# A two-layer transformer kernel: free distances between the stages of a written-out order, and stacking transfers issued by GpSimd

## The chip, the core and the metric

The kernel runs on one core of a Trainium2 chip. The metric is the device time of one execution in microseconds (us). TensorE multiplies matrices, VectorE and ScalarE do elementwise work, SyncE issues nearly all the transfers, and GpSimd does very little in the kernel before. In the profile these are PE (with PEld for its weight loads), DVE, ACT, SP and POOL.

## What is computed

The reference is a transformer of two layers on a sequence of 256 tokens with 1024 features, all in float32. Per layer:

```python
h = _rmsnorm(x, norm_attn[layer]); proj = h @ w_in[layer]      # 1024 x 2956
o_sb = stick_breaking_attention(...)     # 4 heads
o_mb = moba_attention(...)               # 4 heads
o_ns = nsa_attention(...)                # 4 heads: compressed, selected and window branch
o_df = diff_attention(...)               # 4 heads, difference of two softmaxes
x = x + concatenate([o_sb, o_mb, o_ns, o_df]) @ w_out[layer]
h2 = _rmsnorm(x, norm_mlp[layer])
x = x + square(relu(h2 @ w_up[layer])) @ w_down[layer]         # 1024 x 4096 x 1024
```

and a last norm after both layers.

## The kernel before, in words

**Precision.** A float32 number is split into a high part, rounded to the fast matmul type, and the low part that is left. A product takes three matmuls: high by high, high by low, low by high. Each weight piece of 1 MB is loaded into a buffer (`wraw`, three of them), split by ScalarE (`whi`) and VectorE (`wlo`), in halves, and multiplied.

**Stages of a layer** (`attention`, lines 1137 to 1193; `out_proj` 1225; `mlp` 1251). Six projections (`proj`: vg, sqk, nqk, dqk, v2, mqk) come one after another, and the four kinds of attention (`stick`, `nsa`, `diff`, `moba`) are woven between them, one unit of work per head. Each unit is cut into stages by `yield`: scores, softmax, transposes, product with V, split for the output product. Then come `out_proj` (four pieces of `w_out`) and the MLP, 16 rounds of up and down.

**Stacking.** Scores need a high and a low part of 64 rows stacked on the 128 partitions, or other arrangements of them. `stack2` (lines 896 to 902) makes one by four transfers from SBUF to SBUF, 64 partitions by 2 KB each, issued by SyncE: three stacks after sqk (12 transfers), one after nqk (4), three after mqk (12), so 28 a layer and 56 in all. `stack3` (line 883), for `diff`, goes through HBM and stays on SyncE.

**The order is written out beforehand.** No call goes to the machine directly. `Order.note` records each with a clock (`at` sets it), `link` finds what depends on what, and `schedule` (lines 348 to 459) plays the program through a small model of the engines (a cost for each operation from `estimate`, line 212) in which every engine takes, of the calls that are ready, the one with the lowest clock. The order that comes out is what each engine's queue gets, and each queue runs in that order. So the clocks are priorities: `START` (line 27) for the units of each head, `LOADS` and `LEADS` for loading and splitting each weight piece, `FIRST` for the first norm, and `STAGE = 1.2`, by which `run` (line 848) raises the clock from one stage of any unit to the next. `choose` (line 360) lets SyncE's next call block its queue when its buffer isn't free.

**Start.** SyncE loads x, the identity and the gains, and then the first weights. GpSimd sets a few constants. `setup_consts`, `setup_bias` and `setup_small` (lines 562 to 626) load small tables at the clock of the projection that they stand beside.

**The compressed branch.** `compress` (line 1004) leaves one tile `VC` of 128 x 64 whose four groups of 32 partitions hold the same values; in `nsa` (line 1099) head h multiplies 32 partitions of it with 32 partitions of `PcT`, a product that uses 32 rows of the array.

Of the kernel before, what the change touches and what calls it, by code (L numbers as in the profile page):

```python
# [26 lines left out]
START = {  # L27
    "sb": ((-2128.1, -135.2, -1435.8, 37.9), (-286.7, -731.7, -641.4, 39.7)),
    "ns": ((27.1, -1051.7, 53.8, 45.5), (48.2, -2101.2, 32.8, -175.5)),
    "cw": ((-1062.2,), (-2120.7,)),  # L30
    "cmp": ((-1801.8,), (-695.1,)),
    "df": ((-1887.0, -3174.2, -1854.8, -2205.7), (24.0, -2246.5, 53.7, 52.7)),
    "mb": ((-87.3, -1433.6, -45.1, -356.5), (-276.0, -1568.2, -350.0, -7140.8)),
}

LOADS = (
# [6 lines left out]
)  # L43
LEADS = (
# [17 lines left out]
)  # L62
CW_LOAD = 41.5
STAGE = 1.2

FIRST = (-100.5, -617.1)
# [63 lines left out]
GAP, DRAIN = 13.0, 94.0  # L130

SLOW_RATE = 200.0

WINDOW, BUSY_COLUMNS = 10240 / 3, 3060
LOOK_AHEAD, MARGIN = 0.75, 1.0
SPARE = {"ps": 2}

# [40 lines left out]
class Order:  # L178
# [33 lines left out]
    def estimate(op, eng, method, writes, reads):  # L212
        o, n = writes[0], _columns_of(writes[0])
        if method == "dma_start":
            op.bytes = 4 * n * o.ap[0][1]
            if _space(o) == SBUF and (_space(reads[0]) == SBUF or "scratch" in reads[0].tensor.name) and o.ap[0][1] <= 64:
                op.bytes *= DMA_RATE / SLOW_RATE
            return 650.0 if _space(o) == _space(reads[0]) == SBUF else 475.0
# [129 lines left out]
    def schedule(self):  # L348
# [9 lines left out]
        dma, now = 0.0, 0.0  # L358

        def choose(e):  # L360
            skipped, pick = [], None
            while ready[e] and pick is None:
# [7 lines left out]
                if ok and not self.buffers(op, held):  # L370
                    ok = False
                    if e == "SP":
                        skipped.append(x)
                        break
# [36 lines left out]
        while len(done) < len(ops):  # L411
# [9 lines left out]
            for e in ENGINES:  # L421
# [8 lines left out]
                if op.bytes:  # L430
                    dma = max(dma, op.end + DMA_START) + op.bytes / DMA_RATE
                    op.end = dma + DMA_SEEN
# [51 lines left out]
def trunk(ctx: ExitStack, tc: tile.TileContext, x, w_in, w_out, w_up, w_down, gattn, gains, pos, cw1, cw2,  # L484
# [50 lines left out]
    nc.sync.dma_start(gn, gains)  # L535
    for f in range(2):
        nc.sync.dma_start(xs[:, 1, f * 512:(f + 1) * 512], xv[:, 1, f * 512:(f + 1) * 512])
    at(-100.0)

    half = cp.tile([128, 1], F32, name="half")  # L540
# [5 lines left out]
    negone = cp.tile([128, 128], F32R, name="negone")  # L546
    nc.gpsimd.memset(F(negone), -1.0)
# [5 lines left out]
    KC = [cp.tile([128, 2, 16], F32R, name=f"KC{i}") for i in range(2)]  # L553
    w2 = cp.tile([128, DEPTH, 2, 2, 64], F32, name="w2")
# [832 lines left out]
```

## Time and profile before

| | |
|---|---|
| median of 3 runs | 649.02 us (647.96 to 649.22) |
| the profiled execution | 648.43 us, of which the span from first to last instruction is 646.7 us |
| PE busy | 622.2 us, 96% of the span |
| DVE, ACT, POOL busy | 441.7, 358.9 and 8.3 us |
| DMA | 126.94 MB, 196 GB/s on average |

The span is that of the profiled execution, and the 1.73 us around it are taken as fixed. A matmul's end is modelled, so that short pauses between matmuls do not show as idle time: busy time is an upper bound of the work. A busy array isn't an array at its peak either.

### The profile page before, as it was taken

What the parts mean: (1) busy time and instruction counts of PE and PEld (TensorE: products, weight loads), DVE (VectorE), ACT (ScalarE), POOL (GpSimd) and SP (SyncE); (2) the same over time, 40 slices, a digit from 0 to 9 for tenths busy, and PEclk for the clock granted to TensorE, in tenths of its full rate; (3) what the DMA queues carried; (4) which work ended last, traced back from release to release, by engine and by line L of the source; (5) the groups of instructions that cost most, each with busy time, mean ns of one, the idle gap of its engine ahead of it and who ended that gap; (6) DMA issues with size and microseconds to landing.
All of it is one profiled execution on the core that took longest, in us unless ns stands there. A gap on an engine that the chain in (4) does not pass through costs nothing.

```text
span 646.7 us, 9744 instructions
## 1 busy us (share of the span) xinstructions
PE 622.2 (96%) x3674; PEld 529.0 (82%) x3674; DVE 441.7 (68%) x900; ACT 358.9 (56%) x693; POOL 8.3 (1%) x25
## 2 busy tenths in 40 slices
PE   5989999999999999999999999999999999999995
PEld 4978768788888888888889977887788888888885
DVE  5749579779576566556686674998866666576466
ACT  5547587566455454445364774776744454454453
POOL 2010000000000000000000000000000000000000
PEclk9999999999999999999999999999999999999999
DMA  7787955844354465555636958446355555545531
GB/s 275 254 246 227 273 196 222 255 148 176 122 215 155 176 256 186 199 192 196 212 112 222 276 222 235 190 126 236 127 196 195 196 199 191 197 162 196 196 130 66
DMA packets 26895, 126.94 MB, mean 196 GB/s; under 512 B 3880, under 2 KB 5928, under 8 KB 14048
## 3 DMA queue, kind: packets, MB, share of 16 engines
q1 hardware_dynamic: 26848, 126.32, 57.0%
q8 instruction: 29, 0.48, 0.3%
q14 instruction: 18, 0.15, 0.1%
HBM read 115.79 MB, written 3.17 MB: 184 GB/s over the span
## 4 chain that ended last, share of the span: by engine, by line
PE 75%; DMA 9%; DVE 8%; ACT 5%; issue 1%; SPq 1%; POOLq 0%; POOL 0%; ACTq 0%; DVEq 0%
PE ps L480 75%; DMA wraw<-in_w_in_dram 3%; DVE wlo L480 3%; DVE t L480 2%; ACT t L480 2%; ACT whi L480 2%; DMA wraw<-in_cw_dram 2%; DVE xs L480 1%; DMA cst<-in_cst_dram 1%; DMA s<-qtl 1%; DMA wraw<-in_w_down_dram 1%; DVE x L480 1%; SPq L480 1%; DMA t<-bias_scratch 1%; ACT x L480 1%
## 5 line engine op out<-in xcount | busy, mean ns | idle before, releaser
L480 DVE TENSOR_TENSOR wlo<-wraw,whi 128x1024 fp32r<-128x1024 f32 (+1 forms) x192 | 231.2, 1212 | 109.6 <-ACT whi L480 93.7
L480 ACT ACTIVATE whi<-wraw 128x1024 fp32r<-128x1024 f32 (+1 forms) x192 | 199.8, 1049 | 147.0 <-PE ps L480 111.3
L480 PE MATMUL ps<-x,whi 128*128 128x256 f32 (+1 forms) x1024 | 212.7, 341 | 0.7 <-DVE x L480 0.7
L480 PEld LDWEIGHTS ps<-x,whi 128*128 128x128 f32 x1024 | 153.8, 190 | 15.9 <-issue 1.2
L480 PE MATMUL ps<-whi,t 128*128 128x512 f32 (+1 forms) x528 | 162.6, 385 | 0.3 <-ACT whi L480 0.3
L480 PEld LDWEIGHTS ps<-x,wlo 128*128 128x128 f32 x768 | 112.9, 190 | 12.0 <-issue 0.6
L480 PE MATMUL ps<-x,wlo 128*128 128x256 f32 x768 | 122.0, 283 | 0.1
L480 PEld LDWEIGHTS ps<-whi,t 128*128 128x128 f32 x528 | 97.8, 188 | 20.1 <-ACT whi L480 1.0
L480 PE MATMUL ps<-wlo,t 128*128 128x512 f32 (+1 forms) x264 | 101.0, 385 | 0.0
L480 ACT ACTIVATE t<-ps 128x256 f32<-128x256 f32 (+1 forms) x109 | 44.1, 413 | 45.9 <-PE ps L480 45.1
L480 PEld LDWEIGHTS ps<-wlo,t 128*128 128x128 f32 x264 | 49.7, 188 | 9.5 <-DVE wlo L480 0.2
L480 ACT ACTIVATE t<-t 128x512 fp32r<-128x512 f32 (+5 forms) x53 | 29.3, 552 | 35.4 <-DVE t L480 33.6
L480 ACT ACTIVATE t<-t,sm 128x128 f32<-128x128 f32 (+1 forms) x98 | 42.2, 443 | 10.7 <-DVE sm L480 10.4
L480 DVE TENSOR_TENSOR t<-ps,t 128x256 f32<-128x256 f32 x64 | 26.7, 421 | 28.0 <-ACT t L480 27.3
L480 PE MATMUL ps<-whi,x 128*128 128x512 f32 (+1 forms) x128 | 36.0, 384 | 1.0 <-ACT x L480 1.0
L480 DVE TENSOR_TENSOR t<-t,t 128x512 fp32r<-128x512 f32 (+2 forms) x44 | 27.4, 622 | 8.0 <-ACT t L480 6.9
L480 DVE CUSTOM_DVE_ANT_0 t<-ps,Bt 128x256 f32<-128x256 f32 (+1 forms) x80 | 24.4, 352 | 9.0 <-PE ps L480 9.0
L480 PEld LDWEIGHTS ps<-whi,x 128*128 128x128 f32 x128 | 23.1, 193 | 4.7 <-ACT x L480 1.5
L480 PE MATMUL ps<-whi,mixh 128*128 128x512 f32 (+1 forms) x68 | 26.7, 397 | 0.0
L480 PE MATMUL ps<-whi,mixl 128*128 128x512 f32 (+1 forms) x68 | 26.5, 389 | 0.0
L480 PE MATMUL ps<-wlo,mixh 128*128 128x512 f32 (+1 forms) x68 | 26.3, 386 | 0.0
L480 DVE SCALAR_TENSOR_TENSOR t<-t 128x512 f32<-128x512 f32 (+1 forms) x36 | 22.9, 635 | 1.0
(139 smaller groups left out, 475.1 us busy)
## 6 DMA issues: line engine op xcount, KB each, us to landing
wraw<-in_w_up_dram SPq DMA_DIRECT2D x32, 1024.0 KB, 4.8
wraw<-in_w_down_dram SPq DMA_DIRECT2D x32, 1024.0 KB, 4.8
wraw<-in_w_in_dram SPq DMA_DIRECT2D x20, 1024.0 KB, 4.9
wraw<-in_cw_dram SPq DMA_DIRECT2D x8, 1024.0 KB, 9.4
wraw<-in_w_out_dram SPq DMA_DIRECT2D x8, 1024.0 KB, 6.6
s<-qth SPq DMA_DIRECT2D x28, 128.0 KB, 4.3
s<-qtl SPq DMA_DIRECT2D x28, 128.0 KB, 3.2
wraw<-in_w_in_dram SPq DMA_DIRECT2D x4, 792.0 KB, 6.7
```

Source lines behind the costliest of these rows:

```text
L480: fn(*a, **k)
```

## The change

1. All the clocks are replaced by new ones. Instead of one `STAGE` for all, `STAGES` gives a distance, of either sign, for each stage of each head of each kind and layer. `CW_LOAD` has one value a layer, and `SETUP` gives the small loads distances of their own.
2. `stack2` issues its transfers on GpSimd's queue.
3. The model: a DMA issue on GpSimd costs 1000 ns (on SyncE 650 ns for one inside SBUF), each issuing engine has a DMA queue of its own, the least gap between matmuls is 14 ns, and SyncE may look past four calls whose buffers aren't free.
4. Eleven matmuls of `negone` with zeros stand at the head of PE's queue; `negone` and the zeros are set by VectorE.
5. `VC` becomes a tile of four blocks, block h zero outside of partitions 32h to 32h+31, so that the product takes all 128 rows; four copies make it instead of one.

```diff
-CW_LOAD = 41.5
-STAGE = 1.2
+CW_LOAD = (41.5, 48.9)
+
+STAGES = {
+    "sb": (((108.7, -127.7, 154.5, 212.1, 2.6), (56.3, -117.1, -134.2, 119.8, 55.1), (-73.1, 224.1, -250.0,
...
+}
+
+SETUP = (
+    -43.2, -25.2, -92.3, -41.0, -227.3, 245.8, 3.6, 22.9, -207.8,
+)
...
-GAP, DRAIN = 13.0, 94.0
+GAP, DRAIN = 14.0, 94.0
...
+POOL_DMA = 1000.0
...
+WARM = 11
...
+        if method == "dma_start" and eng == "POOL":
+            op.bytes = 4 * n * o.ap[0][1] * DMA_RATE / SLOW_RATE
+            return POOL_DMA
...
-        dma, now = 0.0, 0.0
+        dma, now = dict.fromkeys(ENGINES, 0.0), 0.0
...
-                    if e == "SP":
+                    if e == "SP" and len(skipped) == 4:
                         skipped.append(x)
                         break
...
-                    dma = max(dma, op.end + DMA_START) + op.bytes / DMA_RATE
-                    op.end = dma + DMA_SEEN
+                    dma[e] = max(dma[e], op.end + DMA_START) + op.bytes / DMA_RATE
+                    op.end = dma[e] + DMA_SEEN
...
+    at(-1000.0)
+    negone = cp.tile([128, 128], F32R, name="negone")
+    nc.vector.memset(F(negone), -1.0)
+    at(-100.0)
...
+    at(-1000.0)
+    p, w = ps_att(), t2(F32R)
+    nc.vector.memset(F(w), 0.0)
+    for i in range(WARM):
+        mm(p, negone, w, i == 0, i == WARM - 1)
+    at(-100.0)
...
+    VC = cp.tile([128, 4, 64], F32, name="VC")
+    nc.gpsimd.memset(VC, 0.0)
...
-    def setup_consts():
+    def setup_consts(clock):
+        at(clock, SETUP[0])
         nc.sync.dma_start(c, cst)
...
-    def setup_bias():
+    def setup_bias(clock):
+        at(clock, SETUP[2])
         tb = ap.tile([32, 12], F32, name="tb")
...
-        for _ in unit(h):
-            clock += STAGE
+        for s, _ in enumerate(unit(h)):
+            clock += STAGES[name][l][h][s]
             at(clock)
...
-                nc.sync.dma_start(F(s[64 * m:64 * m + 64, i]), F(x[order[m]][64 * i:64 * i + 64]))
+                nc.gpsimd.dma_start(F(s[64 * m:64 * m + 64, i]), F(x[order[m]][64 * i:64 * i + 64]))
...
-        VC = ap.tile([128, 64], F32, name="VC", tag="VC", bufs=2)
-        evac(VC, p[:, 0:64])
-        return VC, clock
+        for h in range(4):
+            r = slice(32 * h, 32 * h + 32)
+            evac(VC[r, h], p[r, 0:64])
+        return clock
...
-            av.append((VCs[0][32 * h:32 * h + 32], PcT[32 * h:32 * h + 32], 0))
+            av.append((VC[:, h], PcT, 0))
...
```

## Rows read from the trace of the kernel before

**Rows 1.** The page: busy time by engine, and the chain by engine.
```profile
PE 622.2 (96%) x3674; PEld 529.0 (82%) x3674; DVE 441.7 (68%) x900; ACT 358.9 (56%) x693; POOL 8.3 (1%) x25
...
PE 75%; DMA 9%; DVE 8%; ACT 5%; issue 1%; SPq 1%; POOLq 0%; POOL 0%; ACTq 0%; DVEq 0%
```
**Rows 2.** Busy time of the engines in stretches: attention, MLP, attention, MLP.
```profile
7.40:148.30 140.90, 135.76 (x931) 114.54 (x931) 105.14 (x311) 92.70 (x233) 3.30 (x7) 1.00 0.72 234
148.30:326.40 178.10, 178.10 (x908) 151.09 (x909) 115.06 (x148) 86.13 (x119) 0.55 (x1) 1.00 0.51 185
326.40:461.80 135.40, 130.28 (x930) 112.11 (x928) 101.74 (x284) 89.10 (x215) 0.55 (x1) 1.00 0.65 209
461.80:638.70 176.90, 176.60 (x898) 150.00 (x899) 113.43 (x143) 86.81 (x121) 0.55 (x1) 1.00 0.47 170
```
**Rows 3.** Waits of PE over the span: us in total, times, longest.
```profile
PE ps L480 <- DVE xn L480: 7.4, 1, 7.4
PE ps L480 <- DMA s<-qtl: 2.6, 3, 1.3
PE ps L480 <- DMA wraw<-in_cw_dram: 1.3, 2, 0.7
PE ps L480 <- DVE xs L480: 1.2, 2, 0.6
PE ps L480 <- ACT t L480: 1.0, 1, 1.0
PE ps L480 <- DMA t<-in_hot_dram: 1.0, 1, 1.0
PE ps L480 <- ACT x L480: 1.0, 1, 1.0
```
**Rows 4.** PE's timeline at the first weights: start, us in all, count.
```profile
11.23 1.01 PE L480 MATMUL ps<-whi,x 128*128 128x396 f32 x2
...
14.13 0.88 PE L480 MATMUL ps<-whi,x 128*128 128x396 f32 x4
14.85 0.52 PE L480 MATMUL ps<-wlo,x 128*128 128x396 f32 x2
```
**Rows 5.** Stacking transfers over the span: ns of an issue (least, median, most), and landing.
```profile
L480 SPq DMA_DIRECT2D s<-qth x28: 461/588/607, 33.6 to 434.5; - x28
L480 SPq DMA_DIRECT2D s<-qtl x28: 462/596/1412, 36.2 to 437.6; - x28
...
DMA to landing us min/median/max: 2.2/3.9/7.8
```
**Rows 6.** SyncE's queue at the last group of twelve stacking transfers.
```profile
430.07 1.11 SPq L480 DMA_DIRECT2D s<-qth  x2
...
435.15 3.00 SPq L480 DMA_DIRECT2D s<-qtl  x4
438.25 0.53 SPq L480 DMA_DIRECT2D wraw<-in_w_out_dram  x1
```
**Rows 7.** PE's timeline around there, a product of `VC` (32*64) among it.
```profile
427.15 0.65 PE L480 MATMUL ps<-PcT,VC 32*64 32x256 f32 x4
427.73 0.55 PE L480 MATMUL ps<-ident,t 128*128 128x128 f32 x3
...
438.86 0.47 PE L480 MATMUL ps<-s,s 128*128 128x256 f32 x2 [1.27 <-DMA s<-qtl]
```
**Rows 8.** Groups of POOL: its longest instruction, and a short one.
```profile
L480 POOL CAST msb<-cst 128x256 fp32r<-128x256 f32 x1 | 1.4, 1395 | 0.0
...
L480 POOL MEMSET Bc<- 128x128 f32 x1 | 0.2, 204 | 0.0
```
**Rows 9.** Groups of DVE by shape: splitting weights, and scaling by a column.
```profile
L480 DVE TENSOR_TENSOR wlo<-wraw,whi 128x1024 fp32r<-128x1024 f32 x184 | 223.6, 1222 | 107.9 <-ACT whi L480 92.3 <-PE ps L480 15.2
...
L480 DVE TENSOR_SCALAR t<-t,sm 128x256 f32<-128x256 f32 x25 | 8.5, 349 | 0.1
```
**Rows 10.** The copy that makes `VC`: ns, and its start.
```profile
L480 DVE COPY VC<-ps x1: 219/219/219, 408.1 to 408.1; 128x64 f32<-128x64 f32 x1
```

More of the change, by code (lines that the diff above doesn't have):

```diff
@@ L27 @@
 START = {
[L28 to L33, printed above, removed]
+    "sb": ((-248.9, -199.3, -114.1, -39.1), (-78.6, -144.2, -73.5, -49.7)),
+    "ns": ((-244.9, -201.1, 58.0, 43.6), (34.4, -250.0, -4.8, -16.4)),
+    "cw": ((-111.2,), (-138.7,)),
+    "cmp": ((-199.7,), (-197.7,)),
+    "df": ((-250.0, -232.6, -136.2, -184.4), (16.1, -237.3, 58.0, -100.2)),
+    "mb": ((-250.0, -63.5, -250.0, -176.1), (-36.2, -249.7, -131.0, -248.6)),
 }
 LOADS = (
[6 rows of a table removed]
[6 rows of a table added]
 )
 LEADS = (
[17 rows of a table removed]
-)
-CW_LOAD = 41.5
-STAGE = 1.2
-FIRST = (-100.5, -617.1)
[17 rows of a table added]
+)
+CW_LOAD = (41.5, 48.9)
+STAGES = {
[7 rows of a table added]
+    "cmp": (((111.1, 39.1, 250.0, -250.0, 250.0),), ((-136.0, -178.1, -245.4, 226.4, 250.0),)),
[7 rows of a table added]
+}
+SETUP = (
+    -43.2, -25.2, -92.3, -41.0, -227.3, 245.8, 3.6, 22.9, -207.8,
+)
+FIRST = (-7.7, -250.0)
 LAYER = 300.0
@@ L535, in trunk @@
     nc.sync.dma_start(gn, gains)
+    at(-100.0, SETUP[8])
     for f in range(2):
         nc.sync.dma_start(xs[:, 1, f * 512:(f + 1) * 512], xv[:, 1, f * 512:(f + 1) * 512])
+    at(-100.0)
+    at(-1000.0)
+    negone = cp.tile([128, 128], F32R, name="negone")
+    nc.vector.memset(F(negone), -1.0)
     at(-100.0)
@@ L545, in trunk @@
     nc.gpsimd.memset(G, 0.0)
-    negone = cp.tile([128, 128], F32R, name="negone")
-    nc.gpsimd.memset(F(negone), -1.0)
+    at(-1000.0)
[4 more added lines that the diff above has]
+    at(-100.0)
     tri = cp.tile([128, 128], F32R, name="tri")
@@ L568, in setup_consts @@
             nc.gpsimd.tensor_copy(KC[i], Pc[:, 0, 0, :].rearrange("p (a b) -> p a b", a=2))
+        at(clock, SETUP[1])
         for l in range(DEPTH):
@@ L587, in setup_bias @@
         nc.sync.dma_start(rt, rows)
+        at(clock, SETUP[3])
         p = ps_att()
@@ L593, in setup_bias @@
         nc.sync.dma_start(scr, vb[:12])
+        at(clock, SETUP[4])
         for g in range(6):
@@ L601, in setup_bias @@
             nc.vector.tensor_copy(Bt[:, 2 * g:2 * g + 2, :], rev)
+        at(clock, SETUP[5])
         nc.gpsimd.memset(Bc, 8.0 * NEG)
@@ L604, in setup_bias, with setup_small @@
         nc.vector.tensor_copy(Bc[:, 0, :, 0:7], Bt[:, 4:8, 159:256:16])
-    def setup_small():
+    def setup_small(clock):
+        at(clock, SETUP[6])
         lv = t2()
         nc.sync.dma_start(lv[:, :DEPTH * 128], lamv.to_broadcast([128, DEPTH * 128]))
+        sl = small(2)
+        nc.sync.dma_start(sl, subln)
+        at(clock, SETUP[7])
         d = small(4)
@@ L621, in setup_small @@
                                            e[:, 2 * l + 1:2 * l + 2], op0=ALU.add, op1=ALU.subtract)
-        sl = small(2)
-        nc.sync.dma_start(sl, subln)
         for l in range(DEPTH):
@@ L1151, in attention @@
         if l == 0:
-            setup_consts()
+            setup_consts(clock)
+            at(clock)
         acc, clock = proj(l, "sqk", xT, False, clock)
@@ L1160, in attention @@
         if l == 0:
-            setup_bias()
+            setup_bias(clock)
+            at(clock)
         acc, clock = proj(l, "nqk", xT, False, clock)
@@ L1168, in attention @@
         if l == 0:
-            setup_small()
+            setup_small(clock)
+            at(clock)
         acc, clock = proj(l, "dqk", xT, False, clock)
@@ L1175, in attention @@
         at(clock)
-        VC, _ = compress(l, base + START["cw"][l][0], base + CW_LOAD)
+        compress(l, base + START["cw"][l][0], base + CW_LOAD[l])
         at(clock)
-        VCs[:] = [VC]
         run(cmp, l, "cmp", 0)
@@ L1193, in attention @@
         return mix, clock
-    VCs = []
     def ps_out():
```

59 rows, old and new, of tables (LEADS, LOADS, STAGES) are left out of this document.

## The prediction

> **What bounds the kernel now.** I read the page first. PE is busy for 622.2 of 646.7 us and three quarters of the chain are PE's [rows 1], so only what PE loses can be won, and the 24.5 us in which it shows idle are the first measure of that. POOL, with 8.3 us of work [rows 1], is nearly free to issue transfers.
>
> Next the stretches [rows 2]. The two MLPs run for 178.1 and 176.9 us with 0.0 and 0.3 us of PE idle: the change alters no instruction there, and I give it nothing. The two attention stretches, each with its output product, run 931 and 930 matmuls in 140.9 and 135.4 us, with PE idle for 5.1 us in each. So the same work takes 5.5 us longer in the first layer. Before the first stretch lie 7.4 us in which PE waits for the norm of x, after the last MLP about 8 us of last norm and store; the change touches neither wait.
>
> The waits of PE [rows 3] tell what the idle time is. Waits for `xs` and for the norm's `x` (1.2 and 1.0 us) belong to the boundaries between stages, where nothing else is ready, and stay. What an order or a queue can move is the wait for stacked parts (2.6), for the compression's weights (1.3), for a score's evacuation (1.0) and for the table of buckets (1.0): 5.9 us, and some 0.7 us of smaller ones, so 6.6 us. To this come pauses inside "busy" time, since a matmul's modelled end hides short ones.
>
> The starts of the first matmuls show the clock [rows 4]. From 11.23 to 14.13 eight matmuls of 396 columns start in 2.90 us, 0.36 each; the next four take 0.72 us, 0.18 each. That is 1.2 GHz against 2.4 GHz: PE, idle until 7.41, ran the first 6.7 us of its work at half speed.
>
> **The change part by part.** The sum is made against the profiled execution, 648.43 us; the median of the runs is 0.6 us above it, which I add at the end.
>
> *Eleven matmuls at the start.* 512 columns at half speed are 0.36 x 512/396 = 0.47 us, so 5.1 us in all, beginning once VectorE has written two constants (about 1.3 us after the start, since nothing else waits on VectorE before x lands). They end at about 6.4, before PE is wanted at 7.41, and cost nothing; if they began 1 us later they would begin to. [...] The eight matmuls then need 1.44 instead of 2.90 us, a gain of 1.5 at most there, but ScalarE and VectorE are still splitting x in this stretch. Bounds 0 and 2.9 (the eight, and as much again for transposes before them); I take 0.7, half of the first 1.5.
>
> *Transfers on GpSimd's queue.* Removed from SyncE are 56 issues of 0.59 us [rows 5], 33 us of its time. SyncE isn't short of time, but its queue runs in order: the last group of twelve takes from 430.07 to 438.25, and the load of `w_out` goes out only behind it [rows 6]. Twelve issues also make a chain of 8.2 us, at whose end PE stands still for 1.27 us [rows 7]. On GpSimd the trace before shows no issue. Its instructions take from 0.20 to 1.40 us [rows 8], and the longest stacking issue on SyncE took 1.41 [rows 5], so I bound an issue by 0.2 and 1.4 us. The change's own model puts it at 1000 ns against 650 on SyncE; the ratio times the measured 0.59 gives 0.91, an assumption and no measurement, and it lies inside. I take 0.9. A group of twelve then takes 10.8 us and its last part lands 3.7 us later, counted from the split. Three of the four groups have other matmuls to cover this; the last has none (the wait of 1.27 us is there), and moving the mqk projection ahead in the new order should give most of it back. Cost 1 us, bounds 0 and 3.7. GpSimd's other work (constants, the power in each norm) would queue behind a transfer that waits for its split; the norms stand at the boundaries, far from the groups, and the constants are early, so I count 0, and up to 1 us if that cover fails.
>
> The Trainium skill (DMA: Bandwidth & Descriptors, "Issuing engines are not separate DMA queues") speaks against this part: transfers from all issuers share the same engines, and another issuer only saves the time to initiate. By that rule the queue of its own would give nothing beyond those 33 us of a queue that has slack; the trace agrees in so far as the wait of 1.27 us ends on landing. The same page gives a start-up of about 1 us for GpSimd's path against 0.6 us; by that price each group would land 0.4 us later, an estimate from that page.
>
> *Free distances, free small loads, a SyncE that looks further.* The clocks are only priorities, so the price must come from what PE loses. Of the 6.6 us of movable waits I take three quarters, 5.0 us: the 1.0 us for the bucket table was bound to the clock of its projection and now isn't, and weights no longer queue behind stacking. Of the 5.5 us by which the first layer is longer, the clock accounts for about 1.5; half of the remaining 4 makes 2.0. For pauses that don't show no row gives a price: bounds 0 and 5.1 us a layer (as much as shows), and I take 0.9 a layer, near the lower end, because the order before already fills every longer gap; 1.8 in all. Below, each term could be a loss, since an order fixed in advance turns a misjudged price into a wait; that is the last rival.
>
> *The larger `VC`.* Four matmuls in the shape 32*64 take 427.15 to 427.73 [rows 7], and there are four such groups. In the shape of their neighbours they need no change of shape on entering: between 0 and 0.3 us a group, 0.6 in all. Three more copies a layer of 0.22 us at most [rows 10] lie on ScalarE or VectorE well before the first use (the copy at 408.1, the product at 427.15), and are hidden.
>
> *Sum.* 0.7 - 1.0 + 5.0 + 2.0 + 1.8 + 0.6 = 9.1 us. 648.43 - 9.1 = 639.3, and with 0.6 about **640 us**.
>
> **The rivals.**
>
> *The stacking queue becomes the wait (slower).* GpSimd makes an issue slow, at 1.4 us. A group of twelve then takes 16.8 us, 8.6 to 9.7 longer than on SyncE. If other matmuls cover 4 us of it in three groups, about 3 x 5.5 + 9 = 25 us stay, of which the new order hides half: 13 lost against 10 won. With half or nothing hidden that is 652 to 664, 656 in the middle. It decides from about 1.2 us an issue. For it: every part of a head's score stands behind one in-order queue, and the order was made for 1.0 us. Against: POOL is empty. What VectorE runs could add to it: splitting weights takes 223.6 us, 1222 ns each, and it runs throughout both stretches [rows 9]. Were each issue held by such an instruction half the time for half its length, 0.3 us would be added, and 0.9 would become 1.2, the point of decision. The Trainium skill has a rule of this kind (SBUF — State Buffer, the "DVE blocks DMA" trap and "Who interferes with whom"): descriptors of a GpSimd transfer can't be written while VectorE runs a two-port mode, which single-input copies and scalings of float32 enter, while two-input operations do not hold them up (inferred there). By that rule only rows like the 25 scalings of 349 ns [rows 9] count, and the delay is small; no row of before can test it. Chance 0.20.
>
> *The first layer is bound by transfers.* Its stretch keeps the DMA engines busy for 0.72 of the time against 0.65 in the second [rows 2]. Then the 2.0 us, and 2.5 of the 5.0, stay, and the result is 644 to 645. For it: PE's waits there are mostly for DMA [rows 3]. Against: they are only 1 us long each. Chance 0.17.
>
> *The distances do nothing.* The model takes whatever is ready, so with few ready calls other priorities give the same order; gains and the cost of the queue cancel, 648 to 650. Against: the clocks are all replaced. Chance 0.06.
>
> *More is won.* All movable waits, all 4 us of the first layer and 3 us a layer of hidden pauses: 6.6 + 4 + 6 + 1.5 = 18, so 631. Chance 0.12.
>
> My forecast has 0.45.
>
> **How the numbers follow.** A measurement here tells about 0.2%, 1.3 us. Faster by more than that are the forecast, the transfer-bound first layer, and the large gain: 0.45 + 0.17 + 0.12 = 0.74, same 0.06, slower 0.20. The range runs from 630, the large gain with its clock term at the upper bound, to 653, into the slow queue near its point of decision; it leaves out most of that rival and little below.
>
> **What would show it.** Right: PE starts near 1.3 us and reaches 0.18 us for 396 columns by about 9; the waits for `s<-qtl`, the bucket table and the compression's weights shrink to under 3 us together; the attention stretches come to about 134 and 132 us while the MLPs stay at 177 to 178; the issues of `s` stand on POOL at about 0.9 us. Wrong: issues on POOL over 1.2 us with PE waiting for `s`; an MLP that changes by over 1 us; a first stretch that stays at 140 with DMA busier; new waits of PE behind weights that another load has overtaken.

## The result, and the profile after

The changed kernel takes 669.23 us (median of 4 runs, 664.57 to 675.58) beside 648.49 for the kernel before in the same session (4 runs): ratio 1.030 [1.024, 1.036], some 20 us slower. The medians count every run, while the ratios leave out three that lie far above the others of their kernel: 675.58 here, 669.41 of the changed order with three loads moved, and 1240.59 of the changed program with all numbers of before. Forecast were 640 and a range from 630 to 653; the sign is that of the first rival. The profiled execution took 672.89 us with a span of 671.1.

The page of the changed kernel, its lines on busy time, on the granted clock and the transfer engines in 40 slices, and on the chain, and last the line on the clock from the page of the kernel before:

```profile
PE 631.8 (94%) x3685; PEld 540.0 (80%) x3685; DVE 442.4 (66%) x896; ACT 363.7 (54%) x705; POOL 40.9 (6%) x81
...
PEclk8996998999999999999999899998999999999998
DMA  8995395653655555555547819683336355554541
...
PE 73%; DMA 14%; DVE 6%; ACT 3%; issue 2%; SPq 1%; POOL 1%; POOLq 0%; ACTq 0%; DVEq 0%
```
```profile
PEclk9999999999999999999999999999999999999999
```

Against [rows 1] the span is 24.4 us longer. PE idles 39.3 us instead of 24.5, and is busy 9.6 us longer, of which the eleven opening matmuls are 4.3 (they run from 1.59 on). Transfers took 14% of the chain instead of 9%. The granted clock is now lower in the fourth slice (6) and the seventh (8), in two of the second attention, and in the first and the last, where before all slices had a 9.

The stretches (columns: us, then busy us and count of PE, PEld, DVE, ACT, POOL, then granted clock, DMA share, GB/s), attention with its output product from 4 us on, MLP, attention, MLP, end:

```profile
4.00:160.60 156.60, 138.97 (x938) 121.00 (x936) 109.84 (x321) 94.63 (x235) 22.05 (x38) 0.92 0.70 217
160.60:338.50 177.90, 177.90 (x911) 151.40 (x912) 116.09 (x149) 87.18 (x120) 0.56 (x1) 1.00 0.52 184
338.50:483.00 144.50, 133.31 (x927) 114.83 (x925) 98.20 (x272) 92.76 (x231) 15.56 (x29) 0.96 0.63 197
483.00:661.90 178.90, 177.82 (x899) 149.63 (x900) 113.19 (x145) 84.91 (x117) 0.39 (x1) 1.00 0.47 168
661.90:671.10 9.20, 1.35 (x12) 1.15 (x10) 4.17 (x11) 2.97 (x7) 0.77 (x2) 0.78 0.30 114
```

Beside [rows 2]: the first attention ends at 160.6 instead of 148.3 (12.3 us later), the second is 144.5 instead of 135.4 long (9.1), the MLPs change by -0.2 and +2.0, the end by +1.2. That is the 24.4. Of the loss 21.4 us sit in the two attention stretches, where the stacks are; why the second MLP takes 2.0 us more was not followed.

The waits of PE (us in all, times, longest):

```profile
PE ps L508 <- DMA s<-qtl: 13.2, 2, 9.6
PE ps L508 <- DMA s<-qth: 4.9, 1, 4.9
PE ps L508 <- DMA st<-parts_scratch: 2.7, 1, 2.7
PE ps L508 <- ACT whi L508: 2.3, 2, 1.3
```

Stacked parts now cost 18.1 us in three waits, where [rows 3] had 2.6 in three. The tile `s`, which the 56 stacking transfers fill, four for each of its buffers; each of these transfers is called a stack below (ns of an issue, least, median, most; first and last start):

```profile
L508 POOL DMA_DIRECT2D s<-qth x28: 518/518/888, 35.4 to 446.6; - x28
L508 POOL DMA_DIRECT2D s<-qtl x28: 518/518/526, 37.8 to 453.3; - x28
...
DMA to landing us min/median/max: 2.2/5.6/14.6
```

The issue that the prediction feared is cheaper on GpSimd than on SyncE, 0.52 against 0.59 us [rows 5]. What grew is the landing: median 5.6 instead of 3.9, longest 14.6 instead of 7.8. The first group of twelve shows it. The timeline of POOL, SyncE's queue and PE there (start, us, count, and in brackets the idle time before and what ended it):

```profile
35.38 2.43 POOL L508 DMA_DIRECT2D s<-qth  x4 [14.58 <-ACT qth L508]
37.80 2.05 POOL L508 DMA_DIRECT2D s<-qtl  x4
41.04 1.03 POOL L508 DMA_DIRECT2D s<-qth  x2 [1.19 <-ACT whi L508]
42.24 0.52 POOL L508 DMA_DIRECT2D s<-qtl  x1 [0.17 <-DVE lam L508]
44.39 0.52 POOL L508 DMA_DIRECT2D s<-qtl  x1 [1.63 <-DMA s<-qth]
...
37.96 0.33 SPq L508 DMA_DIRECT2D wraw<-in_w_in_dram  x1
43.58 0.33 SPq L508 DMA_DIRECT2D wraw<-in_cw_dram  x1
...
44.81 2.08 PE L508 MATMUL ps<-x,whi 128*128 128x256 f32 x16
46.73 0.64 PE L508 MATMUL ps<-x,wlo 128*128 128x256 f32 x4
56.94 1.08 PE L508 MATMUL ps<-s,s 128*128 128x256 f32 x4 [9.57 <-DMA s<-qtl]
...
62.20 0.97 PE L508 MATMUL ps<-x,whi 128*128 128x256 f32 x4
```

SyncE sends one megabyte of weights at 37.96 and another at 43.58, in the midst of the stacks. The stack issued at 42.24 lands at 56.80 by its transfer record, and PE stands from 47.4 to 56.94. Stretches of the same view as above show what the engines and the clock did:

```profile
20.00:46.00 26.00, 26.00 (x212) 26.00 (x211) 16.75 (x36) 11.26 (x16) 7.33 (x14) 1.00 0.96 287
46.00:57.00 11.00, 1.43 (x13) 1.26 (x11) 4.40 (x9) 3.65 (x6) 2.05 (x4) 0.65 0.96 196
57.00:64.00 7.00, 7.00 (x35) 6.45 (x36) 1.56 (x2) 4.37 (x9) 0.00 (x0) 0.58 0.05 15
```

The transfer engines are busy for 0.96 of the time up to the landing. And the wait is paid twice: behind it PE is busy for 7.00 of 7.00 us at a granted clock of 0.58, so most of it ran at the lower level of 1.2 GHz; four matmuls of 256 columns at 62.20 take 0.97 us, 0.24 each, where sixteen at 44.81, before the wait, take 2.08, 0.13 each.

### The profile page after: what moved, and what is told of

Read it like the earlier page. It is cut to its first block, busy times and chain, and to the rows that moved or that the text cites. A ratio compares the mean times of both kernels' runs of the same rounds, so it can differ in the third digit from the quotient of the medians.

```text
span 671.1 us, 9822 instructions
## 1 busy us (share of the span) xinstructions
PE 631.8 (94%) x3685; PEld 540.0 (80%) x3685; DVE 442.4 (66%) x896; ACT 363.7 (54%) x705; POOL 40.9 (6%) x81
## 4 chain that ended last, share of the span: by engine, by line
PE 73%; DMA 14%; DVE 6%; ACT 3%; issue 2%; SPq 1%; POOL 1%; POOLq 0%; ACTq 0%; DVEq 0%
PE ps L508 73%; DMA s<-qtl 4%; DMA st<-parts_scratch 2%; DMA wraw<-in_w_in_dram 2%; DMA wraw<-in_w_down_dram 2%; DVE wlo L508 2%; DMA s<-qth 1%; ACT whi L508 1%; DVE xs L508 1%; DVE t L508 1%; ACT t L508 1%; DMA t<-in_lamv_dram 1%; SPq L508 1%; DMA wraw<-in_w_up_dram 1%; DMA t<-bias_scratch 1%
## 5 line engine op out<-in xcount | busy, mean ns | idle before, releaser
L508 PE MATMUL ps<-x,whi 128*128 128x256 f32 (+1 forms) x1024 | 215.3, 342 | 0.7 <-DVE x L508 0.7
L508 PEld LDWEIGHTS ps<-x,whi 128*128 128x128 f32 x1024 | 156.6, 192 | 16.5 <-DVE x L508 1.1
L508 ACT ACTIVATE t<-ps 128x256 f32<-128x256 f32 (+2 forms) x114 | 46.1, 410 | 40.4 <-PE ps L508 40.1
L508 ACT ACTIVATE t<-t,sm 128x256 f32<-128x256 f32 (+1 forms) x102 | 43.7, 442 | 8.9 <-DVE sm L508 8.6
L508 PE MATMUL ps<-whi,x 128*128 128x512 f32 (+1 forms) x128 | 34.5, 382 | 2.6 <-ACT whi L508 1.3
L508 PE MATMUL ps<-s,s 128*128 128x256 f32 (+1 forms) x64 | 13.0, 338 | 18.1 <-DMA s<-qtl 13.2
L508 POOL TENSOR_TENSOR sm<-sm,half 128x1 f32<-128x1 f32 x6 | 4.0, 663 | 420.7 <-DVE sm L508 420.7
L508 PEld LDWEIGHTS ps<-s,s 128*128 128x128 f32 x64 | 12.0, 255 | 19.9 <-issue 18.8
```

The lines of the kernel that those rows point to most:

```text
L508: fn(*a, **k)
```

## The experiments

All ratios are to the kernel before on the same chip. "Order kept" means that every engine's calls stand as in the kernel named; where the planner runs on other numbers, the whole order is made anew.

**Queue and order, crossed.** First the changed order with its stacks on SyncE:

```diff
-                fn(*a, **k)
+                (self.sync.real.dma_start if op.bytes and op.engine == "POOL" else fn)(*a, **k)
```

> The changed kernel with every engine's order kept as it is; only the 56 stacking transfers are issued by SyncE, at the same place of the written-out order, instead of GpSimd. Sharing theory (two issuers' transfers are served side by side by the same DMA engines, so stacked parts land late behind weight loads issued after them): PE's waits for stacked parts fall from 18.1 us to under 6, and the time from 669 to 648 to 656. Order theory (the new distances are bad by themselves): the waits move elsewhere and the time stays above 662. Path theory (GpSimd's issue or path is slow by itself): as the sharing theory; the third run tells these two apart.

Measured: 664.79 us, 1.027 [1.021, 1.033]; waits for `s<-qtl` 15.1 us. The changed order is slow on the old queue too. Then the order of the kernel before, with the stacks sent to GpSimd when they are issued:

```diff
-                fn(*a, **k)
+                (self.gpsimd.real.dma_start if op.bytes and _space(op.writes[0]) == _space(op.reads[0]) == SBUF else fn)(*a, **k)
```

> The kernel before with every engine's order kept; only the 56 stacking transfers are issued by GpSimd. Sharing theory: stacked parts land later where loads are in flight beside them (first layer and the last group above all), PE's waits for them grow from 2.6 us to 6 to 15, time 653 to 664. Path theory: every group lands later, also where no load is in flight; the same time. Order theory: the queue costs little, 648 to 651.

Measured: 674.68 us, 1.041 [1.039, 1.044]. The queue alone makes a good order 27 us slower, more than any of the three theories gave it. SyncE's queue in the kernel before at the first group, and then the two queues of this one, with the landing of all its stacks:

```profile
33.64 2.45 SPq L480 DMA_DIRECT2D s<-qth  x4
36.19 3.62 SPq L480 DMA_DIRECT2D s<-qtl  x4
40.06 1.23 SPq L480 DMA_DIRECT2D s<-qth  x2
41.39 2.00 SPq L480 DMA_DIRECT2D s<-qtl  x2
...
44.04 0.83 SPq L480 DMA_DIRECT2D wraw<-in_w_in_dram  x2
```
```profile
36.97 5.64 SPq L480 DMA_DIRECT2D wraw<-in_w_in_dram  x2
...
41.10 1.03 POOL L480 DMA_DIRECT2D s<-qtl  x2 [0.29 <-issue]
...
DMA to landing us min/median/max: 2.2/5.7/11.6
```

With both kinds on SyncE, the two weight loads stand behind the twelve stacks and go out from 44.04 on. Without the stacks SyncE reaches the first of them at 36.97, 7 us earlier, and the second at 42.27, and both run beside the stacks.

**Queues by themselves.** A program without the model's computation: groups of 12 stacks of 128 KB on each queue, alone and beside three loads of 1 MB, and GpSimd's group beside VectorE's two kinds of work. Its core, with `eng` the issuing engine:

```python
for n in range(3):
    nc.sync.dma_start(w[n], w_up[0, n])
...
for t in s:
    for m in range(2):
        for i in range(2):
            eng.dma_start(t[64 * m:64 * m + 64, i], q[m][64 * i:64 * i + 64])
```

> A program of its own that leaves out the whole computation and writes nothing of it: groups of the twelve stacking transfers (128 KB each) with nothing else, issued by GpSimd, SyncE or ScalarE, and the same with three weight loads of 1 MB issued by SyncE at the same moment. Sharing theory: alone, a group on GpSimd is done in about the time of one on SyncE (8 to 10 us against 8 to 9); beside loads, a group on GpSimd or ScalarE and the loads finish together, after 13 to 18 us, each load later than the about 9 us for three loads alone, while loads and group in SyncE's one queue finish one after the other. Path theory: the group on GpSimd takes 13 us or more with nothing beside it, and one on ScalarE beside loads stays short. Last, groups on GpSimd beside VectorE at work: if two-port scalings hold up GpSimd's descriptors, that group is late by some us and the one beside subtractions isn't.

Measured, from first issue to last landing: a group alone takes 8.9 us on GpSimd and 9.4 on SyncE and on ScalarE. Three loads alone land 4.8, 7.3 and 9.8 us after their first issue, 2.5 us apart; beside GpSimd's group 5.1, 10.1 and 15.1, so 5.0 apart, and the group needs 17.9. Put behind the loads on SyncE's queue the group needs 17.0, but the loads are there at 4.8, 7.3 and 11.7. Two queues halve each other; in one queue what stands first is held up little, here only the third load, from 9.8 to 11.7. GpSimd's path is not slow by itself. Its queue beside the loads, and the group beside VectorE's scalings and then beside its subtractions:

```profile
27.25 4.07 POOL L528 DMA_DIRECT2D s<-q  x8 [4.10 <-DVE q L538]
35.35 0.52 POOL L528 DMA_DIRECT2D s<-q  x1 [4.02 <-DMA s<-q]
...
213.40 8.91 POOL L528 DMA_DIRECT2D s<-q  x12 [74.41 <-DVE q L538]
229.54 6.10 POOL L528 DMA_DIRECT2D s<-q  x12 [7.23 <-DVE q L538]
```

**The new distances on the old queue**, planned for it:

```diff
-                nc.gpsimd.dma_start(F(s[64 * m:64 * m + 64, i]), F(x[order[m]][64 * i:64 * i + 64]))
+                nc.sync.dma_start(F(s[64 * m:64 * m + 64, i]), F(x[order[m]][64 * i:64 * i + 64]))
```

> The changed kernel with one word changed: stack2 issues on SyncE, and the model that makes the order knows it, so the order is made anew. All other parts of the change (distances, warm start, larger VC, SyncE that looks past four calls) stay. Sharing and path theories: 638 to 652, the distances are worth what I forecast or nothing. Order theory: above 660.

Measured: 661.33 us, 1.024 [1.019, 1.029]. The waits for `s<-qtl` are down to 1.8 us, but many small ones have come, the largest sum 5.6 us, in seven waits for ScalarE's `t`. That could be the distances, or only a fresh order. Four runs with fresh orders followed.

The changed kernel with one transfer timeline for all issuers in its model:

```diff
-                    dma[e] = max(dma[e], op.end + DMA_START) + op.bytes / DMA_RATE
-                    op.end = dma[e] + DMA_SEEN
+                    dma["SP"] = max(dma["SP"], op.end + DMA_START) + op.bytes / DMA_RATE
+                    op.end = dma["SP"] + DMA_SEEN
```

> The changed kernel with one edit in its planner's model: the transfers of all issuers follow one another on a single DMA timeline, as in the kernel before, instead of one timeline for each issuing engine; distances, queue and the rest stay. The order is made anew with it. Theory A (the plan goes wrong because its model lets GpSimd's transfers run beside the weight loads at no cost, so that they land after their planned time): with sharing in the model the long waits for s go, under 6 us in all where the changed kernel had 18, the granted clock comes back to over 0.99, and the time to 650 to 660. Rival B (the distances were chosen for one exact plan, and any other plan made from them loses whatever the model says): waits spread over other tiles as in the run of the new distances on SyncE's queue, 660 to 672. Rival C (GpSimd's queue itself is slow, whatever the plan): waits for s stay over 12 us, 668 to 680.

Measured: 696.78 us, 1.076 [1.072, 1.080], beyond all three theories; the waits for stacks are 3.7 us in all, and 8.8 us of the others are for VectorE's `t`.

The kernel before, its stacks planned for and issued by GpSimd with the changed kernel's model of it:

```diff
-                nc.sync.dma_start(F(s[64 * m:64 * m + 64, i]), F(x[order[m]][64 * i:64 * i + 64]))
+                nc.gpsimd.dma_start(F(s[64 * m:64 * m + 64, i]), F(x[order[m]][64 * i:64 * i + 64]))
```

> The kernel before with its own distances; the stacking transfers are planned for GpSimd's queue and issued there, with the changed kernel's model of it (1.0 us an issue, a DMA timeline of its own); first part at its old clocks. The queue part alone, planned for. Theory A (the model's missing sharing): waits for s over 8 us, clock under 0.985, 660 to 675. Rival B (only the foreign order made the queue costly, 674.7 in the run with before's order kept): 645 to 655 with waits for s under 4 us.

Measured: 688.94 us, 1.063 [1.060, 1.066], again beyond what was expected, with 7.7 us of waits for `s<-qtl`.

The changed program on SyncE's queue with all numbers of before, in essence:

```diff
-CW_LOAD = (41.5, 48.9)
+CW_LOAD = (41.5, 41.5)
...
-GAP, DRAIN = 14.0, 94.0
+GAP, DRAIN = 13.0, 94.0
...
-                    if e == "SP" and len(skipped) == 4:
+                    if e == "SP":
```

> The changed kernel's program (11 opening matmuls, the wider VC, the setup steps split) with the distances, the gap and SyncE's rule of the kernel before, stacks on SyncE. It prices the small parts with a fresh plan from old distances. If distances fit any plan, the small parts' own +0.7 of the clock and +0.6 of VC show: 646 to 649. If any fresh plan loses (rival B of the run with one DMA timeline): 652 to 665, waits spread over many tiles, clock over 0.985.

Measured: 654.44 us, 1.008 [1.006, 1.011]; the loss is spread over short waits, as the second case said.

And the control, the kernel before with one number of its model changed:

```diff
-GAP, DRAIN = 13.0, 94.0
+GAP, DRAIN = 14.0, 94.0
```

> The kernel before with one number of its planner's model changed as in the change, the modelled gap between matmuls from 13 to 14 ns; the program is the same, its order is made anew. A control for what a fresh plan costs by itself. Theory A (the distances hold for nearby plans): 647 to 650. Rival B (the distances fit one exact plan): 653 to 665, with the loss in many short waits of PE and not in transfers of s.

Measured: 678.17 us, 1.049 [1.044, 1.054]. The largest waits of PE behind the first norm's 8.3 us; those for stacked parts are only 2.4 us in all:

```profile
PE ps L480 <- DVE t L480: 4.9, 3, 2.8
PE ps L480 <- ACT whi L480: 3.7, 4, 1.4
PE ps L480 <- DMA wraw<-in_cw_dram: 3.6, 3, 2.0
```

One nanosecond in the model costs 30 us. The distances of before hold for the plan that they belong to and not for its neighbour, and the time of a run in which the planner runs anew says little of the part that was changed. So the 661 us of the new distances on SyncE's queue, and these four, price neither the distances nor the queue; all later runs keep an order.

**What the orders are worth without the stacks' bytes.** Order and issues kept, each stack cut from 512 elements a row to 8, into buffers cleared at the start, so the scores of two families are computed on cleared data:

```diff
...
+                if op.bytes and _space(op.writes[0]) == _space(op.reads[0]) == SBUF:
+                    first = op.writes[0].offset % op.writes[0].ap[0][0] < 512
+                    a = [v[:, 1:2, 44:52] if first else v[:, 0:1, 0:8] for v in a]
                 fn(*a, **k)
```

> The changed kernel with its order on every engine kept, and GpSimd still issuing all 56 stacking transfers at their places; each transfer carries 8 elements a row instead of 512 (2 KB in place of 128 KB) into buffers that were cleared at the start, so the attention's scores for the two families are computed on cleared data. It shows what the changed order is worth when its stacks cost the transfer engines nothing. Theory A (the changed order is sound, and the stacks' bytes beside the weight loads are the loss): PE's waits for s under 2 us in all where the changed kernel had 18, clock over 0.993, 640 to 648. Rival B (the new distances make a slower order in any case): 652 to 662. Rival C (GpSimd's queue is late whatever it carries): waits for s over 10 us, 662 to 672.

> The kernel before with its order kept and the stacks issued by SyncE as ever, each cut to 8 elements a row in the same way, on cleared data. The control for the run before: what the old order gains when the stacks are free. Its waits for s are 2.6 us, so both theories expect 644 to 648; a gain over 4 us would say that the stacks also delay the weight loads behind them on SyncE's queue.

Measured: the changed order 645.45 us, 0.994 [0.991, 0.997]; the old order 644.96, 0.994 [0.992, 0.996]. The largest waits of PE, first in the changed order, then in the old:

```profile
PE ps L528 <- DMA st<-parts_scratch: 3.3, 1, 3.3
PE ps L528 <- DVE t L528: 1.6, 1, 1.6
```
```profile
PE ps L500 <- DVE xn L500: 7.2, 1, 7.2
PE ps L500 <- ACT whi L500: 1.5, 2, 1.2
```

This is the central pair. No wait for a stack is left in either, and the two orders take the same time. The changed kernel's whole loss, 24 us against this run, comes with the stacks' bytes; this pair does not say whether it is by their own time or by the loads beside them. The new distances, the opening matmuls and the rest together gain nothing that shows even when nothing disturbs them.

**The small parts**, on the old order: eleven matmuls put ahead of it, and then the wider `VC` as well, in the calls that the plan has for it.

```diff
+            w, p = self.warm()
+            self.vector.real.memset(w.bitcast(F32), 0.0)
+            for i in range(11):
+                self.tensor.real.matmul(p, w[:, 0:128], w, start=i == 0, stop=i == 10, skip_group_check=True)
             for op in done:
...
+                if op.writes[0].tensor.name.startswith("VC"):
+                    for h in range(4):
+                        r = slice(32 * h, 32 * h + 32)
+                        fn(self.VC[r, h], a[1][r], *a[2:], **k)
```

> The kernel before with its order kept, and 11 matmuls of 512 columns put ahead of it on a cleared tile, as in the change. It prices the warm-up alone. My theory: the first real matmuls run at the full clock, 0.7 us less, 646.5 to 648.5. Rival: nothing is gained or 1 us lost, because the first real matmul waits behind them.

> The run before and the wider VC in the change's way (four evictions into a cleared tile of 4 blocks, the product over 128 rows), the order of the kernel before kept. My theory: 0.6 us less than the run with the warm-up alone, 646 to 648. Rival: the four evictions on the evicting engine delay the softmax behind them and it is 0.5 to 1.5 us slower.

Measured: 649.81 us, 1.002 [1.000, 1.004], and 649.61, 1.003 [1.000, 1.005]. Neither gain shows in the time. For `VC` the trace, beside that of the run with the opening matmuls alone, has one all the same, too small for these intervals: in three of the four groups the first product starts 0.10 us after the matmul before it instead of 0.20, and the two halves of a group are 0.21 apart instead of 0.26, which makes 0.44 us in all.

**Holding SyncE back.** The order of before with stacks on GpSimd once more, but SyncE goes on behind a run of stacks only when GpSimd has issued its last:

```diff
+                stack = op.bytes and _space(op.writes[0]) == _space(op.reads[0]) == SBUF
+                if stack:
+                    fn, held = self.gpsimd.real.dma_start, True
+                elif op.engine == "SP" and held:
+                    f, g = self.flag[0][:, runs:runs + 1], self.flag[1][:, runs:runs + 1]
+                    self.gpsimd.real.memset(f, 0.0)
+                    self.sync.real.dma_start(g, f)
+                    held, runs = False, runs + 1
                 fn(*a, **k)
```

> The kernel before with its order kept and the stacks issued by GpSimd, as in the run that took 674.7; but SyncE now goes on behind each run of stacks only when GpSimd has issued the last of them (GpSimd clears one element behind the run, SyncE copies that element by a small transfer of its own before its next call). So the weight loads keep the place behind the stacks that one in-order queue gave them. Theory A (the second queue costs because SyncE, no longer held by the stacks, sends weight loads ahead and beside them): the loss goes, waits for s under 4 us, 648 to 654. Rival B (GpSimd's own path lands late in the full kernel, loads or not): waits for s stay over 10 us, 665 to 680. Rival C (half and half, the loads that are in flight already when a group starts matter as much): 655 to 665.

Measured: 650.04 us, 1.000 [0.998, 1.002]: all 27 us are gone. SyncE's queue at the first group, and the landing:

```profile
42.55 0.68 SPq L487 DMA_DIRECT2D flag<-flag  x1
43.33 0.35 SPq L489 DMA_DIRECT2D bias_scratch<-t  x1
43.78 1.12 SPq L489 DMA_DIRECT2D wraw<-in_w_in_dram  x2
...
DMA to landing us min/median/max: 2.2/3.6/7.5
```

The loads are back at 43.78, and the landing is a little better than on SyncE. GpSimd's queue was never the fault; that nothing held SyncE's transfers back was. The hold keeps back all of them, the six of the bias table (256 KB each) too; the next run moves the weight loads. The exchange of queues, stacks on SyncE and the 104 weight loads on GpSimd (with them the gains of the last norm, whose buffer has the same name), says it from the other side:

```diff
+                if op.bytes and op.writes[0].tensor.name.startswith("wraw"):
+                    fn = self.gpsimd.real.dma_start
                 fn(*a, **k)
```

> The kernel before with its order kept, stacks on SyncE as ever, and the weight loads (104 of 0.8 or 1 MB) issued by GpSimd instead: the two kinds are again on two queues, but the stacks are on the old one. Theory A (two queues share the engines and the loads run ahead, whichever queue carries which): as with the stacks on GpSimd, waits for s over 8 us, 662 to 685. Rival B (stacks are late because GpSimd issues them): waits for s under 4 us, 646 to 656.

Measured: 712.73 us, 1.098 [1.091, 1.105], further out than expected. The waits and the landing:

```profile
PE ps L482 <- DMA s<-qtl: 19.2, 4, 8.7
PE ps L482 <- DVE xn L482: 13.1, 1, 13.1
PE ps L482 <- DMA st<-parts_scratch: 8.4, 1, 8.4
PE ps L482 <- DMA s<-qth: 6.5, 1, 6.5
...
DMA to landing us min/median/max: 2.2/6.8/13.5
```

Stacks issued by SyncE are late all the same, and here even the wait for the first norm is 13.1 us instead of 7.4 [rows 3]. No run tests the cause, but the trace points to loads beside x: a part of x that goes out at 2.58, behind two loads of GpSimd's at 1.63 and 2.36, lands at 11.92, where the last part of x had landed at 6.87 in the kernel before.

**The same hold in the changed order**, and then three loads moved behind their group.

```diff
+                if op.bytes and op.engine == "POOL":
+                    held = True
+                elif op.engine == "SP" and held:
...
+        late = {n for f, e in zip(firsts, lasts) for n in range(f, e) if done[n].bytes and done[n].engine == "SP"
+                and all(done.index(u) > e for u in done[n].users)}
```

> The changed kernel, order, distances and GpSimd's queue kept, with the same hold: wherever a call of SyncE stands in the order behind a stack, it waits until GpSimd has issued that stack. Theory A (SyncE running ahead is the loss, in this order too): 645 to 653, waits for s under 5 us. Rival B (the changed order itself puts weight loads ahead of and among the stacks, since its planner took the queues for independent, so holding them at their places mends little; on SyncE's queue alone this order took 664.8): 658 to 668, waits for s over 10 us.

> The run before, and the three weight loads that stand among a group of stacks although nothing reads them before the group's end are moved behind its last stack (one load of the compression's weights in each layer, one of the up-projection's). Theory B (loads placed among the stacks by the planner are the loss): 3 to 8 us less than the run before, the waits for s shorter by as much. Rival (these loads are not what the stacks wait behind): within 2 us of the run before.

Measured: 663.56 us, 1.022 [1.017, 1.028], and 664.38, 1.023 [1.017, 1.028]. Here the hold mends 6 us at most (the intervals of 1.030 and 1.022 overlap), as SyncE's queue did (664.79): in this order weight loads stand among the stacks, where its planner, with a `dma[e]` for each issuer, took them for harmless. That these loads are what the held stacks still wait behind is argued, and the traces bear it out in part: PE's waits for `s` shrink from 18.1 us to 9.9 with the hold and to 5.1 with the three loads moved, but now PE waits 5.7 us at one stroke for a moved load, the compression's weights, and the time stays. The other loads are read before their group ends and could not be moved without what reads them.

**Half the stacks on each queue**, order of before, where SyncE's own half still holds its loads back:

```diff
+                if op.bytes and _space(o) == _space(op.reads[0]) == SBUF and o.offset % o.ap[0][0] >= 512:
+                    fn = self.gpsimd.real.dma_start
                 fn(*a, **k)
```

> The kernel before with its order kept; of every two stacks in a row one is issued by SyncE as ever and one by GpSimd, so a group of twelve is issued from two queues side by side, and SyncE still can't run past its own half. If a second queue has a use here, this is it: six issues of 0.59 us instead of twelve on each queue. Theory A (what matters is that the loads stay behind the stacks): no loss, and up to 2 us gained of the 3.5 that free stacks won, 645.5 to 648. Rival (the transfers themselves set the time, not their issues): within 0.2% of the kernel before. Rival (half the hold is not enough, GpSimd's half lands among the loads): 652 to 662.

Measured: 648.93 us over 12 runs, 1.002 [0.999, 1.004]. Twice as many issuers win nothing. No version tried that computes the whole result beats the kernel before.

## Why the prediction was wrong

**The planner's own figure.** A plan is computed on the host when the kernel is built, and the end of its last call can be read from it; it is a plan and no measurement. Set beside the medians:

| order | stacks issued by | plan ends | measured | difference |
|---|---|---|---|---|
| before | SyncE | 634.4 | 648.5 | 14.1 |
| old numbers, warm-up, `VC` | SyncE | 643.7 | 654.4 | 10.7 |
| new distances | SyncE | 651.2 | 661.3 | 10.1 |
| before with the gap at 14 | SyncE | 669.0 | 678.2 | 9.2 |
| after | GpSimd | 631.4 | 669.2 | 37.8 |
| old distances | GpSimd | 650.0 | 688.9 | 38.9 |
| after, one timeline | GpSimd | 667.6 | 696.8 | 29.2 |

A plan for one queue comes true to 9 to 14 us, a plan for two is off by 29 to 39. The changed plan promised 3.0 us; it counted on engines that serve two queues at full rate. That this alone makes the difference isn't shown: the plan with one timeline is off by 29.2 as well. The loss of the control stands in its plan already, which ends 34.6 us later than that of before.

**Transfers on GpSimd's queue (-1.0): the step that failed.** "I take 0.9" priced the issue, which measures 0.52. The landing was carried over unchanged ("its last part lands 3.7 us later"), and that is what broke: 5.6 in the median, 14.6 at most. The error under it is in the first clause, "SyncE isn't short of time, but its queue runs in order": I read the order as an expense. It was what kept the weight loads behind the stacks, and the run with SyncE held back shows that it was worth 27 us in the old order. The cost stood outside my bounds of 0 and 3.7. In the changed order the queue is not all of it: with SyncE held back or issuing the stacks itself 15 to 17 us of loss stay, and by the pair with free stacks they go with the stacks' bytes as well.

**"Weights no longer queue behind stacking"** stood among the gains of the 5.0. In the old order it is the mechanism of the loss; in the changed one it is the likely one, by the waits above, and not proven.

**Distances, 5.0 + 2.0 + 1.8.** Mis-sized: all of it. With free stacks the new order is no faster than the old, 645.45 against 644.96. Of the waits I called movable those for the bucket table and the compression's weights are gone there (those for `s` too, but its stacks are free), and others took their place, 3.3 us for `st` and 1.6 for `t`. The control shows how little such a sum can say: the same program under a plan from a model 1 ns different runs 30 us longer, so pauses in a plan are no reserve that freer numbers must find.

**The clock (0.7) and `VC` (0.6).** The gain of `VC` is there, 0.44 us by the trace, and lost in the noise. The 0.7 is shown by no run. In the run with the opening matmuls alone they start at 1.45 us, but PE then waits 1.3 us for the first transposes and 0.6 within them, and 396 columns reach 0.18 us at 14.4, where before they did at 14.1 [rows 4].

**The rivals.** "The stacking queue becomes the wait" had the sign and the place, PE waiting for `s` behind POOL. Its mechanism, an issue of over 1.2 us, is refuted by 0.52, and its 652 to 664 was short of 669 (the middle of these is 658, and not 656). "The first layer is bound by transfers" named the right resource (DMA share 0.96 around the first group) and took it for a limit to the gain, where it was the loss. Of what I listed as signs of an error two came: PE waited for `s`, and an MLP changed by 2.0 us. The first stretch grew, but its transfer engines were no busier over the whole of it, 0.70 instead of 0.72 [rows 2].

**The shared engines.** Loads land 2.5 us apart alone and 5.0 apart beside stacks of another queue. The Trainium skill ("DMA: Bandwidth & Descriptors", "Issuing engines are not separate DMA queues") says that issuers share the engines, and the trace agrees; I had weighed that as a queue that would give nothing, and not as a loss. The longer start-up that the same page gives for GpSimd's path ("Specifications", first-byte latency) does not show: the shortest landing is 2.2 us from either engine, and a group alone took 8.9 us from GpSimd and 9.4 from SyncE. Twelve issues of GpSimd took 8.91 us beside one-input scalings and 6.10 beside two-input subtractions, 0.74 and 0.51 each. That agrees with the trap in the Trainium skill's "SBUF — State Buffer" ("DVE blocks DMA"); the delay was small here, 0.2 us an issue.

**Waiting and clock.** The two runs of the old order with stacks on GpSimd, free and held, differ by 25.2 us of span. PE is idle for 40.7 and 28.1 us in them and busy for 633.2 and 620.6, at a granted clock of 0.976 and 0.997. So half of the loss is waiting, and half is the same matmuls taking longer; how much of this half is the clock and how much are short pauses is open.

**Open.** Why the exchange of queues costs 63 us and not 37 at most was not followed. Distances searched for SyncE's queue, or for a model in which two queues slow each other, were not tried; the single timeline of one run is not such a model, and its order was worse.

## What to carry to other kernels

Before a transfer is given a queue of its own, ask what its old place in the queue held back: an in-order queue is also a priority, and here the stacks that waited for their data kept the bulk loads from running beside them. A new queue shares the same engines; if the bulk must stay behind, hold it there (here one element copied behind each run of stacks brought 27 us back in the old order, and 6 at most in the new one, whose plan had put loads among the stacks). And where an order comes from a planner, change one thing with the order kept: a fresh plan from the slightest other number cost up to 30 us, more than any part under test.

## What was not expected of the hardware

GpSimd issued a transfer of 64 rows in 0.52 us, faster than SyncE's 0.59, and with eight transfers under way it waited until one had landed: eight go out in 4.07 us at 27.25, the ninth at 35.35 after an idle 4.02 that a landing ended. The transfer records of that program show no more than eight under way for GpSimd at any time, and no more than eight for SyncE and ScalarE taken together: with three loads and five stacks out, SyncE's next stack goes at 61.04, when the first load has landed at 61.03. Two queues were served so evenly that 1.5 MB of stacks and 3 MB of loads each ran at about half their rate (8.9 to 17.9 us, 2.5 to 5.0 us a load), though the loads were issued first. Such a rate per queue can't be seen where only one queue carries bulk, as in the kernel before. And after 9.57 us of idling PE ran for the next 7 us, busy throughout, at a granted clock of 0.58.
